# A mixture-of-experts block: the second expert product turned feature-major, with the last 32 tokens gathered by index

## The chip, the cores and the metric

One core of a Trainium2 chip runs the whole program. The metric is device time in microseconds (us) of one execution; the median of three runs of the kernel before is 1306.14 us (1303.92 to 1308.4).

## The reference, cut to what matters

Two transformer blocks of 256 tokens and 1024 features, all in float32. The first ends in a product-key expert layer: each token picks, in each of 8 heads, 16 of 16384 experts. An expert is a row of `u` and a row of `v`; the token's own features are `xb`.

```python
expert = take_along_axis(cand_i, best_pos)            # t, h, k
gate = softmax(best_s)                                # t, h, k
act = gelu(einsum('thkd,td->thk', u[expert], xb))
return einsum('thk,thkd->td', gate * act, v[expert])
```

The second block reads the sum x + peer_ffn(h): a projection `w_in_2` into five parts, attention, a gated unit, `w_out_2`, two layer norms and a SwiGLU.

## The kernel before

The expert layer is computed densely. An expert is numbered by i (128 values) and j (128 values). The U loop goes over 64 pairs of j. For each j it loads a 512 KB slice of `u`, multiplies it with the 256 normed tokens held feature-major in `h2h`/`h2l` (`fm`, 24 matmuls of 256 columns), applies Gelu and keeps the result in `store0`/`store1` with i on the partitions and the tokens on the free axis. Beside that loop, bit by bit, a list `bg` of steps finds the top 16 of each head (`scores` to `slots`), and from pair 22 on `one_hots` and `g_chunk` build, 8 tokens at a time, the dense gate matrix of those tokens: 16 matmuls in f16, multiplied into the store. There are 32 such chunks.

The V loop then goes over the same 64 pairs of j. For each j it loads a 512 KB slice of `v` (128 experts on the partitions, 1024 features) and adds store-times-v to two PSUM accumulators `acc`, one for each block of 128 tokens. The stored values are the stationary operand and the rows of `v` the moving one: the sum stands token-major, tokens on the partitions.

Every float32 product is made of three matmuls in `mm3` (L101 to L103). A value is split into a high part in float32r and the rest: high by high, high by low, low by high. For a streamed slice the split is done in `load` (L84 to L96): SP starts the DMA into one of four `raw` buffers, ScalarE copies it to `wh` (L94), VectorE subtracts to get `wl` (L95). There are six buffers for `wh` and `wl`, so three slices can be ready. The split of the stored values is in `split` (L127 on ScalarE, L128 on VectorE).

The last four slices of `v` (VLAST) and three slices of `w2` are kept in `held`. After the loop, block 0 is finished first (4 slices, 24 matmuls), added to `x1` on VectorE (L806), transposed on TensorE and split into `xh`/`xl`, while block 1's last 24 matmuls run; then the first quarter of the projection (`tm`, 48 matmuls into `qp`) follows.

Instructions are laid out by a tile framework. Each engine has one queue in order; the framework orders it by program order, with the two conversions in `load` moved ahead by 20 places (`ahead`), and sets all semaphores. GpSimd (POOL) starts no DMA in this kernel and has no work between 196 and 1020 us.

Of the kernel before, what the change touches and what calls it, by code (L numbers as in the profile page):

```python
# [18 lines left out]
P = 128  # L19
# [21 lines left out]
AHEAD = 20  # L41
VLAST = 4
FFIRST = 4
WLAST = 4
# [3 lines left out]
def block_kernel(ctx, tc, a, out):  # L48
# [30 lines left out]

    ahead = [AHEAD_MIX]  # L80


    def load(src, dst=None, parts=1):
# [6 lines left out]
        for i in range(parts):  # L90
            c = slice(i * 1024 // parts, (i + 1) * 1024 // parts)
            nc.sync.dma_start(raw[:, c], src[:, c])
            with tc.high_priority(offset=ahead[0]):
                act.activation(wh[:, c], raw[:, c], AF.Copy)  # L94
                dve.tensor_sub(wl[:, c], raw[:, c], wh[:, c].bitcast(F32))  # L95
        return wh, wl  # L96
# [421 lines left out]
    pp = peer_cm.__enter__()  # L518
    store0 = pp.tile([P, 64, S], F32, tag="store", bufs=2, name="store0")
    work = pp.tile([P, 64, S], F32, tag="store", bufs=2, name="work")  # L520
    wf = work.rearrange("p a b -> p (a b)")
# [23 lines left out]
    eq = wf[:, 0:2048].bitcast(F16).rearrange("p (g a s) -> p g a s", g=16, a=16)  # L545
    fi = carve(256)
    fj = carve(256)
    iota16 = carve(128, F16).rearrange("p (a s) -> p a s", s=TOPK)

    iT = pp.tile([P, S], F16, name="iT")  # L550
    jT = pp.tile([P, S], F16, name="jT")
# [90 lines left out]
    def select(q, half):  # L642
# [8 lines left out]
        for w in (8, 4, 2):  # L651
            dve.tensor_tensor(e[:, :, 0:w], e[:, :, 0:w], e[:, :, w:2 * w], op=ALU.add)
        dve.tensor_tensor(dst.rearrange("p (g s) -> p g s", s=TOPK)[:, g], e[:, :, 0, :],
                          e[:, :, 1, :], op=ALU.add)

    def slots(b):
        pt = bank("ms").rearrange("p (k n) -> p k n", n=P)
# [10 lines left out]
    state = {"pairs": 0, "chunks": 0, "hots": 0}  # L668
    hots = []
    stores = [store0, None]  # L670

    def store_view(j0, n, t):
        s = stores[j0 // 64]
        return s[:, j0 % 64:j0 % 64 + n, t]

    def u_pair():
        jp = state["pairs"]
        if jp == 32 and stores[1] is None:
            stores[1] = pp.tile([P, 64, S], F32, tag="store", bufs=2, name="store1")
        pq = bank_s("mm")  # L680
# [8 lines left out]
        if done < S:  # L689
            act.activation(store_view(2 * jp, 2, slice(done, S)), pq[:, :, done:S], AF.Gelu)  # L690
        state["pairs"] += 1
# [20 lines left out]
    def g_chunk():  # L712
        c = state["chunks"]
        if stores[1] is None:
            stores[1] = pp.tile([P, 64, S], F32, tag="store", bufs=2, name="store1")
        ea, el, eb = hots.pop(0)
# [30 lines left out]
    bg += [(4, lambda q=q, h=h: select(q, h)) for h in range(2) for q in range(2)]  # L747
    bg += [(0, lambda: slots(0)), (2, lambda: slots(1))]
    total = sum(w for w, _ in bg)
# [15 lines left out]

    acc = [pair() for _ in range(NB)]
    held = pp.tile([P, 16, 1024], F32R, tag="store", bufs=2, name="held2")

    def v_mm(j, unit, sp, jj, b):
# [7 lines left out]
    xh, xl = across()  # L777
    late = []
    for jp in range(npairs):
        sv = store_view(2 * jp, 2, slice(0, S))  # L780
        if 2 * (npairs - jp) <= VLAST:
            o = 2 * VLAST + npairs - jp - 1
            sp = held[:, o, :].rearrange("p (q j t) -> p q j t", q=2, t=S)
        else:
            sp = pp.tile([P, 2, 2, S], F32R, tag="e", bufs=2, name="sp")
        ph, pl = sp[:, 0], sp[:, 1]
        split(ph, pl, sv)
        for jj in range(2):
            j = 2 * jp + jj
            n = 128 - j - 1  # L790
            if n >= VLAST:
                unit = load(a["v"][j])
                for b in range(NB):
                    v_mm(j, unit, (ph, pl), jj, b)
            else:
                late.append((j, load(a["v"][j], (held[:, 2 * n], held[:, 2 * n + 1])), (ph, pl), jj))
    w2 = a["w2"]
    n = 2 * VLAST + VLAST // 2
    first_q = [load(w2[i], (held[:, n + 2 * i], held[:, n + 2 * i + 1]) if i < 3 else None)
               for i in range(4)]  # L800
    for b in range(NB):
        for item in late:
            v_mm(*item, b)
        for half in range(2):
            c = slice(512 * half, 512 * half + 512)
            dve.scalar_tensor_tensor(x1[:, b, c], acc[b][:, half, :], 1.0 / GSCALE, x1[:, b, c],  # L806
                                     op0=ALU.mult, op1=ALU.add)
        transposed_split(x1[:, b], xh, xl, b, KD)
    qp = pair()
    for b in range(NB):  # L810
        for i in range(4):
            tm(first_q[i], 2 * i, [qp[:, 0, :], qp[:, 1, :]], xh, xl, blocks=[b])
    peer_cm.__exit__(None, None, None)
# [438 lines left out]
```

## Time and profile before

| what | value |
|---|---|
| median of 3 runs | 1306.14 us (1303.92 to 1308.4) |
| the profiled execution, its own time | 1306.18 us |
| its span, from the first to the last instruction | 1304.3 us |
| TensorE busy | 1279.4 us, 98% of the span |
| VectorE busy / ScalarE busy | 853.0 us, 65% / 708.9 us, 54% |
| GpSimd busy | 29.7 us, 2% |
| moved by DMA | 229.12 MB, mean 176 GB/s |
| granted TensorE clock, mean | 0.996 of 2.4 GHz |

A busy TensorE is not yet one at its peak, since matmuls overlap and the ends of their records are modelled. What a matmul costs is read from the distance between the starts of neighbours in the timeline. A group's mean duration (389 ns for a matmul of 512 columns) is longer than that distance and must not be added up.

### The profile page before, as it was taken

How to read it: one execution, taken by the hardware profiler on the slowest of the kernel's cores; microseconds unless marked ns; L12 is line 12 of the kernel's file. 1: busy time of each engine (PE TensorE's matmuls, PEld its weight loads, DVE VectorE, ACT ScalarE, POOL GpSimd, SP SyncE). 2: the span in 40 equal slices, each digit the busy share in tenths (PEclk: the TensorE clock that was granted, in tenths of full speed). 3: DMA queues.
4: the chain of work that ended last, by engine and by line, in shares of the span. 5: the costliest groups of instructions: out<-in, count | busy, mean ns of one | idle time of the engine just before them, and what ended most of it. 6: DMA issues, size and time to landing. Idle time of an engine off the chain costs nothing. (4 is left out here: it accounts for less than half of the span.)

```text
span 1304.3 us, 21924 instructions
## 1 busy us (share of the span) xinstructions
PE 1279.4 (98%) x8644; PEld 1164.7 (89%) x8644; DVE 853.0 (65%) x1454; ACT 708.9 (54%) x1167; POOL 29.7 (2%) x40
## 2 busy tenths in 40 slices
PE   8999999999999999999999999999999999999997
PEld 7998989999999999999988888888887887899996
DVE  5656685499987777777655555555556687554556
ACT  6555454444568777777544444544444475344443
POOL 2200000000000000000000000000000110000000
PEclk9989999999999999999999999999999999999999
DMA  8523555555555444454555565555556564355552
GB/s 301 193 67 99 177 193 182 178 162 162 167 162 190 152 162 158 162 162 162 179 193 194 194 194 193 194 193 194 193 194 216 194 219 137 114 192 180 193 182 94
DMA packets 65479, 229.12 MB, mean 176 GB/s; under 512 B 8288, under 2 KB 9056, under 8 KB 65248
## 3 DMA queue, kind: packets, MB, share of 16 engines
q1 hardware_dynamic: 64800, 226.54, 52.5%
q8 instruction: 68, 1.11, 0.3%
q10 hardware_dynamic: 576, 1.18, 0.3%
q14 instruction: 35, 0.29, 0.1%
HBM read 226.64 MB, written 1.05 MB: 175 GB/s over the span
## 5 line engine op out<-in xcount | busy, mean ns | idle before, releaser
L95 DVE TENSOR_TENSOR wl<-raw,wh 128x1024 fp32r<-128x1024 f32 (+1 forms) x385 | 469.2, 1221 | 322.8 <-ACT wh L94 321.5
L94 ACT ACTIVATE wh<-raw 128x1024 fp32r<-128x1024 f32 (+1 forms) x385 | 405.1, 1054 | 434.3 <-PE ps_lg L102 211.8
L101 PE MATMUL ps_mm<-xh,wh 128*128 128x256 f32 x1408 | 401.8, 285 | 0.0
L103 PE MATMUL ps_mm<-xh,wl 128*128 128x256 f32 x1408 | 398.6, 283 | 2.1 <-DVE wl L95 2.1
L102 PE MATMUL ps_mm<-xl,wh 128*128 128x256 f32 x1408 | 398.3, 283 | 0.0
L103 PEld LDWEIGHTS ps_mm<-xh,wl 128*128 128x128 f32 x1408 | 269.9, 192 | 2.7 <-DVE wl L95 2.7
L102 PEld LDWEIGHTS ps_mm<-xl,wh 128*128 128x128 f32 x1408 | 270.1, 192 | 0.7
L101 PEld LDWEIGHTS ps_mm<-xh,wh 128*128 128x128 f32 x1408 | 269.8, 192 | 0.7
L101 PE MATMUL ps_lg<-wh,sp 128*128 128x512 f32 x496 | 193.0, 389 | 0.0
L102 PE MATMUL ps_lg<-wl,sp 128*128 128x512 f32 x496 | 193.0, 389 | 0.0
L103 PE MATMUL ps_lg<-wh,sp 128*128 128x512 f32 x496 | 192.9, 389 | 0.0
L103 PEld LDWEIGHTS ps_lg<-wh,sp 128*128 128x128 f32 x496 | 93.1, 188 | 19.5
L101 PEld LDWEIGHTS ps_lg<-wh,sp 128*128 128x128 f32 x496 | 93.1, 188 | 19.3
L102 PEld LDWEIGHTS ps_lg<-wl,sp 128*128 128x128 f32 x496 | 93.1, 188 | 19.2
L705 ACT ACTIVATE oh<-oh,gL 128x128 f16<-128x128 f16 x256 | 83.6, 429 | 2.2 <-DVE oh L703 1.9
L101 PE MATMUL ps_mm<-hh,wh 128*128 128x256 f32 x192 | 56.5, 294 | 0.0
L103 PE MATMUL ps_mm<-hh,wl 128*128 128x256 f32 x192 | 55.7, 290 | 0.3 <-DVE wl L95 0.3
L102 PE MATMUL ps_mm<-hl,wh 128*128 128x256 f32 x192 | 55.1, 287 | 0.0
L128 DVE TENSOR_TENSOR sp<-store,sp 128x512 fp32r<-128x512 f32 x62 | 42.4, 683 | 0.2 <-ACT sp L127 0.2
L127 ACT ACTIVATE sp<-store 128x512 fp32r<-128x512 f32 x62 | 38.0, 613 | 0.4 <-DVE store L732 0.4
L101 PEld LDWEIGHTS ps_mm<-hh,wh 128*128 128x128 f32 x192 | 37.4, 195 | 1.0 <-DVE gates L402 0.4
L103 PEld LDWEIGHTS ps_mm<-hh,wl 128*128 128x128 f32 x192 | 37.3, 195 | 0.8 <-DVE wl L95 0.7
(387 smaller groups left out, 1679.0 us busy)
## 6 DMA issues: line engine op xcount, KB each, us to landing
raw<-in_u_dram SPq DMA_DIRECT2D x128, 512.0 KB, 3.3
raw<-in_v_dram SPq DMA_DIRECT2D x128, 512.0 KB, 3.3
raw<-in_wgu_dram SPq DMA_DIRECT2D x44, 512.0 KB, 3.3
raw<-in_wa_dram SPq DMA_DIRECT2D x32, 512.0 KB, 4.2
raw<-in_wd_dram SPq DMA_DIRECT2D x22, 512.0 KB, 3.3
raw<-in_w_dram SPq DMA_DIRECT2D x20, 512.0 KB, 4.4
raw<-in_wo_dram SPq DMA_DIRECT2D x16, 512.0 KB, 3.8
raw<-in_wq_dram SPq DMA_DIRECT2D x16, 512.0 KB, 4.3
```

What stands on the lines that cost most here:

```text
L94: act.activation(wh[:, c], raw[:, c], AF.Copy)
L95: dve.tensor_sub(wl[:, c], raw[:, c], wh[:, c].bitcast(F32))
L101: pe.matmul(dst, lh, rh, start=start, stop=False)
L102: pe.matmul(dst, lh, rl, start=False, stop=False)
L103: last_mm[0] = pe.matmul(dst, ll, rh, start=False, stop=stop)
L127: act.activation(dh, src, AF.Copy)
L128: dve.tensor_sub(dl, src, dh.bitcast(F32))
L705: act.activation(el[:, t // 2, :, t % 2], ea[:, t // 2, :, t % 2], AF.Copy, scale=gL[:, GT * c + t:GT * c + t + 1])
```

## The change

The dense path now covers tokens 0 to 223 (NT = 224). The last 32 (NR) go another way from the Gelu on; the U product is still made for all 256.

- **V loop, turned round.** For each j and each of 8 blocks of 128 features (d) there are two matmuls in place of twelve over two token blocks: `wh` of that block is the stationary operand and the moving one is high and low part of the 224 tokens side by side (448 columns); then `wl` is stationary and the high part alone moves (224 columns). The sums stand feature-major in eight PSUM banks, columns 0 to 223 and 224 to 447, and use all of PSUM.
- **U loop.** 28 chunks in place of 32. One more Gelu for each pair, of the last 32 tokens, into `last_u`; every fourth pair ScalarE starts a DMA of it to a buffer in HBM, `kept_u` (16 DMAs).
- **New steps in the list.** `row_numbers` (VectorE) computes the 4096 expert numbers of the 32 tokens, GpSimd moves them with 4 DMAs into an order in which each partition holds one token's 32 slots, VectorE reads them back. `across_x1` transposes `x1` into `x1T` (16 transposes, 4 ScalarE copies).
- **Gather.** During the V loop GpSimd issues 32 indexed DMAs of 128 x 32 values from `kept_u` and 32 indexed DMAs of 128 rows of `v` (512 KB each). VectorE picks the values and weighs them (`weigh`, 4 times 3 instructions), then multiplies and adds each row into `rows_sum` (`add_row`, 32 instructions of 128x1024). All of these VectorE instructions are queued behind the last `wl` of their pair (`issue_after`).
- **End.** For each d: one float32 matmul of 32 columns brings `rows_sum` into columns 448 to 479 of the bank, eight matmuls of the four kept slices follow, then two ScalarE copies, two VectorE instructions and a split. No transposes are needed before the projection; after its first quarter 16 transposes bring `x1` back token-major. The `w2` slices are no longer kept in `held`.

```diff
+NT = 224
+NR = S - NT
+ROWS = 4
+U_FIRST = 5
+V_FIRST = 18
+V_LAST = 60
...
+    def row_numbers():
+        t = slice(P, 2 * P)
...
+        dve.scalar_tensor_tensor(pack[:, 0, :], fj[:, t], float(NKEYS), fi[:, t], op0=ALU.mult,
+                                 op1=ALU.add)
...
+            pool.dma_start(prep[r], pack[P - NR:P, :, r])
+        dve.tensor_copy(index, prep[:, 0:2, :])
...
     def u_pair():
...
+        act.activation(last_u[0][:, 2 * k:2 * k + 2, :], pq[:, :, NT:S], AF.Gelu)
+        if k == 3:
+            act.dma_start(kept_u[:, 2 * jp - 6:2 * jp + 2, :], last_u[0])
...
-        nch = S // GT
+        nch = NT // GT
...
-    acc = [pair() for _ in range(NB)]
...
+    def fetch_u(c):
+        at_u = pp.tile([P, 8, NR], F32, tag="last_u", bufs=2, name="at_u")
+        for i in range(8):
+            r = 8 * c + i
+            pool.indirect_dma_start(at_u[:, i, :], None, table,
+                                    bass.IndirectOffsetOnAxis(ap=index[:, 1, r:r + 1], axis=0))
...
+    def fetch_row(r):
+        pool.indirect_dma_start(place(r), None, vrows,
+                                bass.IndirectOffsetOnAxis(ap=index[:, 0, r:r + 1], axis=0))
+
+    def add_row(r):
...
+            dve.scalar_tensor_tensor(rows_sum, place(r), share[:, r:r + 1], rows_sum,
+                                     op0=ALU.mult, op1=ALU.add)
+
+    def steps(jp):
+        if jp == 0:
+            fetch_u(0)
+            fetch_u(1)
+        for c in range(4):
+            if jp == U_FIRST + 3 * c:
+                weigh(c)
+                if c < 2:
+                    fetch_u(c + 2)
...
+        for r in range(NR):
+            if jp == V_FIRST + r * (V_LAST - V_FIRST) // NR:
+                add_row(r)
+                if r + ROWS < NR:
+                    fetch_row(r + ROWS)
...
+    acc = [bank("ms"), bank("ms"), lgs[0][:, 0, :], lgs[0][:, 1, :], lgs[1][:, 0, :],
+           lgs[1][:, 1, :], bank("mm"), bank("mm")]
...
+    def v_mm(j, unit, sp, d):
         wh, wl = unit
-        t = slice(b * P, b * P + P)
-        for half in range(2):
-            c = slice(512 * half, 512 * half + 512)
-            mm3(acc[b][:, half, :], sp[0][:, jj, t], sp[1][:, jj, t], wh[:, c], wl[:, c],
-                j == 0, j == 127)
+        c = slice(P * d, P * d + P)
+        pe.matmul(acc[d][:, 0:2 * NT], wh[:, c], sp.rearrange("p q t -> p (q t)"), start=j == 0,
+                  stop=False, skip_group_check=True)
+        pe.matmul(acc[d][:, 0:NT], wl[:, c], sp[:, 0], start=False, stop=j == 127,
+                  skip_group_check=True)
...
+        with tc.issue_after(last_wl[0]):
+            steps(jp)
...
+    for d in range(KD):
+        c = slice(P * d, P * d + P)
+        pe.matmul(acc[d][:, 2 * NT:2 * NT + NR], rows_sum[:, c], mine, start=False, stop=True,
+                  skip_group_check=True)
+        for item in late:
+            v_mm(*item, d)
...
+        dve.tensor_tensor(both[:, 0:NT], both[:, 0:NT], acc[d][:, 0:NT], op=ALU.add)
+        dve.scalar_tensor_tensor(y, both, 1.0 / GSCALE, y, op0=ALU.mult, op1=ALU.add)
+        split(xh[:, d, :], xl[:, d, :], y)
```

## Rows read from the trace of the kernel before

**Rows 1.** The page: the span, the busy time of each engine, and the granted TensorE clock in 40 equal slices.

```profile
span 1304.3 us, 21924 instructions
PE 1279.4 (98%) x8644; PEld 1164.7 (89%) x8644; DVE 853.0 (65%) x1454; ACT 708.9 (54%) x1167; POOL 29.7 (2%) x40
PEclk9989999999999999999999999999999999999999
```

**Rows 2.** The table by stretch. Columns: the stretch and its length, busy us of each engine with its instructions, granted clock, DMA share, GB/s. In order: the top-k part of the U loop, the end of the U loop, the V loop, the end of the expert layer, the start of the program.

```profile
300.00:400.00 100.00, 97.87 (x835) 97.01 (x834) 88.96 (x285) 56.67 (x97) 0.00 (x0) 1.00 0.53 171
...
600.00:640.00 40.00, 40.00 (x367) 39.83 (x366) 29.70 (x38) 25.61 (x54) 0.00 (x0) 1.00 0.53 171
...
652.30:989.60 337.30, 337.30 (x1490) 279.28 (x1489) 191.96 (x189) 166.88 (x190) 0.00 (x0) 1.00 0.59 196
984.00:1000.00 16.00, 14.31 (x68) 11.73 (x67) 11.56 (x11) 9.08 (x9) 0.00 (x0) 1.00 0.87 310
0.00:33.00 33.00, 27.73 (x173) 24.93 (x174) 19.70 (x38) 22.88 (x40) 7.67 (x12) 1.00 0.84 297
```

**Rows 3.** TensorE's timeline (start us, us of one, operation): the last slice of the U loop (21 matmuls from the first of these rows to the second), the first matmul of the V loop, the first after it.

```profile
649.78 0.28 PE L101 MATMUL ps_mm<-xh,wh 128*128 128x256 f32 x1
...
652.18 0.28 PE L103 MATMUL ps_mm<-xh,wl 128*128 128x256 f32 x1
652.30 0.40 PE L101 MATMUL ps_lg<-wh,sp 128*128 128x512 f32 x1
...
989.60 0.39 PE L101 MATMUL ps_lg<-held 128*128 128x512 f32 x1
```

**Rows 4.** TensorE's timeline where the moving operand is short: 64 columns in float32 (24 in a row), 128 columns in float32 (6 in a row), and 128 columns in float32r (the attention logits, two matmuls at a time on 64 partitions each; nine steps from the first of these two rows to the last).

```profile
1067.62 2.79 PE L999 MATMUL ps_lg<-v,ptt 128*128 128x64 f32 x24
...
212.95 0.83 PE L573 MATMUL ps_ms<-work 128*128 128x128 f32 x6
...
1034.12 0.27 PE L152 MATMUL ps_lg<-qkL,qkH 64*128 64x128 f32 x2
...
1035.12 0.27 PE L152 MATMUL ps_lg<-qkL,qkH 64*128 64x128 f32 x2
```

**Rows 5.** TensorE's timeline across one chunk of the gate matrix in the U loop, 16 matmuls in f16, with its neighbours.

```profile
542.58 0.28 PE L103 MATMUL ps_mm<-xh,wl 128*128 128x256 f32 x1
542.70 0.23 PE L719 MATMUL ps_lg<-oh 128*128 128x128 f16 x1
...
543.57 0.22 PE L721 MATMUL ps_lg<-oh 128*128 128x128 f16 x1
...
543.80 0.28 PE L102 MATMUL ps_mm<-xl,wh 128*128 128x256 f32 x1
```

**Rows 6.** TensorE's timeline across four transposes and the second matmul after them.

```profile
206.33 0.60 PE L562 MATMUL ps_ms<-ident,qtok 128*128 128x128 f32 x4
...
206.89 0.28 PE L102 MATMUL ps_mm<-xl,wh 128*128 128x256 f32 x1
```

**Rows 7.** Groups by line in the V loop, 652.3 to 989.6 us: count, busy us, mean ns of one, and the idle time of the engine before them with what ended it.

```profile
L95 DVE TENSOR_TENSOR wl<-raw,wh 128x1024 fp32r<-128x1024 f32 x122 | 149.5, 1226 | 143.7 <-ACT wh L94 143.7
L94 ACT ACTIVATE wh<-raw 128x1024 fp32r<-128x1024 f32 x122 | 129.5, 1061 | 168.8 <-PE ps_lg L102 167.0 <-PE ps_mm L102 1.8
...
L128 DVE TENSOR_TENSOR sp<-store,sp 128x512 fp32r<-128x512 f32 x60 | 41.0, 683 | 0.0
```

**Rows 8.** Single lines elsewhere (ns of one: least, median, most): a VectorE multiply-add with both operands in SBUF, and the two halves of a split of 256 columns.

```profile
L1038 DVE SCALAR_TENSOR_TENSOR xc<-x,lst,l1g x4: 736/742/746, 1100.1 to 1113.3; 128x512 f32<-128x512 f32 x4
...
L127 ACT ACTIVATE f<-sg x18: 398/398/420, 1141.4 to 1286.0; 128x256 fp32r<-128x256 f32 x18
...
L128 DVE TENSOR_TENSOR f<-sg,f x18: 417/421/426, 1142.7 to 1286.5; 128x256 fp32r<-128x256 f32 x18
```

**Rows 9.** TensorE's timeline at the end of the expert layer: the last matmul before the wait, the transposes of block 0 with the wait before them, the first matmul of `qp`, the first after `qp`.

```profile
996.63 0.39 PE L102 MATMUL ps_lg<-held 128*128 128x512 f32 x1
998.70 0.65 PE L135 MATMUL ps_ms<-ident,x 128*128 128x128 f32 x4 [1.69 <-DVE x L806]
...
1003.30 0.39 PE L101 MATMUL ps_lg<-held,xh 128*128 128x512 f32 x1
...
1015.21 0.39 PE L101 MATMUL ps_lg<-wh,xh 128*128 128x512 f32 x1
```

**Rows 10.** ScalarE's and VectorE's timelines just after the U loop: the last pair leaves its PSUM bank.

```profile
653.34 0.58 ACT L686 ACTIVATE ps_mm<-ps_mm 128x512 f32<-128x512 f32 x1
...
654.61 0.68 DVE L688 TENSOR_TENSOR store<-store,ps_mm 128x512 f32<-128x512 f32 x1
```

**Rows 11.** DMAs: a slice of `v` and a piece of the output (size, median us from issue to landing), and the time that SP takes to issue one slice (ns, least, median, most).

```profile
raw<-in_v_dram SPq DMA_DIRECT2D x128, 512.0 KB, 3.3
...
out_dram<-ot SPq DMA_DIRECT2D x4, 256.0 KB, 2.1
...
L92 SPq DMA_DIRECT2D raw<-in_v_dram x128: 327/328/328, 637.5 to 982.8; - x128
```

**Rows 12.** GpSimd's timeline: two of its instructions on tiny operands.

```profile
28.07 2.10 POOL L264 TENSOR_TENSOR hst<-hst,neghalf 128x5 f32<-128x5 f32 x1
...
188.72 0.56 POOL L142 TENSOR_TENSOR st<-st,neghalf 128x1 f32<-128x1 f32 x1 [110.64 <-DVE st L141]
```

More of the change, by code (lines that the diff above doesn't have):

```diff
@@ L747, in block_kernel @@
     bg += [(4, lambda q=q, h=h: select(q, h)) for h in range(2) for q in range(2)]
-    bg += [(0, lambda: slots(0)), (2, lambda: slots(1))]
+    bg += [(1, row_numbers), (0, lambda: slots(0)), (2, lambda: slots(1))]
+    bg += [(0, lambda b=b: across_x1(b)) for b in range(NB)]
     total = sum(w for w, _ in bg)
@@ L764, in block_kernel @@
             g_chunk()
[L766 to L777 removed]
+    table = kept_u.rearrange("p j t -> (p j) t")
@@ new lines, in block_kernel @@
+    vrows = a["v"].rearrange("j i d -> (j i) d")
+    places = [h2pool.tile([P, 2, 1024], F32, tag=t, name="rows") for t in ("xh", "xl")]
+    fetched = []
+    def fetch_u(c):
[4 more added lines that the diff above has]
+                                    bass.IndirectOffsetOnAxis(ap=index[:, 1, r:r + 1], axis=0))
+        fetched.append(at_u)
@@ new lines, in weigh, with place @@
+    def weigh(c):
+        at_u = fetched[c]
+        r = slice(8 * c, 8 * c + 8)
+        dve.tensor_tensor(at_u, at_u, mine[:, None, :].to_broadcast([P, 8, NR]), op=ALU.mult)
+        dve.tensor_reduce(share[:, r], at_u, axis=AX.X, op=ALU.add)
+        dve.tensor_tensor(share[:, r], share[:, r], prep[:, 2, r], op=ALU.mult)
+    def place(r):
+        return places[r % ROWS // 2][:, r % 2, :]
+    def fetch_row(r):
+        pool.indirect_dma_start(place(r), None, vrows,
+                                bass.IndirectOffsetOnAxis(ap=index[:, 0, r:r + 1], axis=0))
@@ new lines, in block_kernel @@
+    lgs = [pair() for _ in range(2)]
+    acc = [bank("ms"), bank("ms"), lgs[0][:, 0, :], lgs[0][:, 1, :], lgs[1][:, 0, :],
+           lgs[1][:, 1, :], bank("mm"), bank("mm")]
+    held = pp.tile([P, 14, 1024], F32R, tag="store", bufs=2, name="held2")
+    def v_mm(j, unit, sp, d):
+        wh, wl = unit
+        c = slice(P * d, P * d + P)
[3 more added lines that the diff above has]
+                  skip_group_check=True)
@@ L792, in block_kernel @@
                 unit = load(a["v"][j])
-                for b in range(NB):
-                    v_mm(j, unit, (ph, pl), jj, b)
-            else:
-                late.append((j, load(a["v"][j], (held[:, 2 * n], held[:, 2 * n + 1])), (ph, pl), jj))
+                for d in range(KD):
+                    v_mm(j, unit, sp[:, jj], d)
+            else:
+                late.append((j, load(a["v"][j], (held[:, 2 * n], held[:, 2 * n + 1])), sp[:, jj]))
+        with tc.issue_after(last_wl[0]):
+            steps(jp)
@@ L797, in block_kernel @@
+    xh, xl = across()
     w2 = a["w2"]
-    n = 2 * VLAST + VLAST // 2
-    first_q = [load(w2[i], (held[:, n + 2 * i], held[:, n + 2 * i + 1]) if i < 3 else None)
-               for i in range(4)]
-    for b in range(NB):
[L802 to L812, printed above, removed]
+    for d in range(KD):
+        c = slice(P * d, P * d + P)
[3 more added lines that the diff above has]
+            v_mm(*item, d)
+        y = x1T[:, d, :]
+        both = pp.tile([P, S], F32, tag="last_u", bufs=2, name="both")
+        act.activation(both[:, 0:NT], acc[d][:, NT:2 * NT], AF.Copy)
+        act.activation(both[:, NT:S], acc[d][:, 2 * NT:2 * NT + NR], AF.Copy)
+        dve.tensor_tensor(both[:, 0:NT], both[:, 0:NT], acc[d][:, 0:NT], op=ALU.add)
+        dve.scalar_tensor_tensor(y, both, 1.0 / GSCALE, y, op0=ALU.mult, op1=ALU.add)
+        split(xh[:, d, :], xl[:, d, :], y)
@@ L813, in block_kernel @@
+    qp = pair()
+    for i in range(4):
+        tm(load(w2[i]), 2 * i, [qp[:, 0, :], qp[:, 1, :]], xh, xl)
+    for b in range(NB):
+        for g in range(2):
+            pt = bank_t("ms")
+            for i in range(4):
+                pe.transpose(pt[:, i, :], x1T[:, 4 * g + i, b * P:b * P + P], ident)
+            act.activation(x1[:, b, 512 * g:512 * g + 512].rearrange("p (k n) -> p k n", n=P), pt,
+                           AF.Copy)
     peer_cm.__exit__(None, None, None)
```

63 lines of the change are left out of this document (49 added, 14 removed).

## Prediction

> **What bounds the kernel now.** I read the page first: TensorE is busy 98% of the span, VectorE 65%, ScalarE 54%, GpSimd 2%, and the granted clock is 9 or more tenths of full speed in all slices but one [rows 1]. So time is gained only where TensorE has fewer or shorter matmuls, and lost where it begins to wait. The table by stretch says the same of each stage: in the V loop TensorE is busy for all of 337.3 us, VectorE for 57% of it, ScalarE for 49%, and the DMA engines for 0.59 [rows 2]. What TensorE pays for a matmul is read from the starts in its timeline. The V loop runs 124 slices of 12 matmuls between 652.30 and 989.60 us [rows 3]: 2.720 us a slice, 226.7 ns for 512 columns. The U loop runs 20 steps between 649.78 and 652.18 us [rows 3]: 120.0 ns for 256 columns. A line through both has 0.4167 ns a column (which is 2.4 GHz, the clock granted there) and 13.3 ns for each matmul. In the groups by line VectorE and ScalarE sit idle for 144 and 169 us in the V loop, and what ends this idleness is TensorE giving a `wh`/`wl` buffer back [rows 7]. Nothing there is late for TensorE.
>
> **Part 1, the V loop.** Per slice 12 matmuls of 512 columns go; 8 of 448 and 8 of 224 columns come: 5376 streamed columns in place of 6144, but 16 weight loads in place of 12. The 448-column matmul lies between the two measured sizes: 448 x 0.4167 + 13.3 = 200.0 ns. The 224-column one lies below both, and the next weights must be in by then. The line alone gives 106.7 ns. 64 columns in float32 take (2.79 - 0.27)/23 = 109 ns, 128 take (0.83 - 0.27)/5 = 112 ns (0.27 us is the length of one record), and the float32r logits of 128 columns 1.00/9 = 111 ns a step [rows 4]. Half the columns are not cheaper, while f16 with 128 columns takes 0.87/15 = 58 ns [rows 5]. So there is a floor near 110 ns under 32-bit matmuls that is not their columns; I read it as the weight load. From above the 256-column matmul bounds it, 120.0 ns. I take 112, the row nearest in size that shows the floor. A slice is then 8 x (200.0 + 112) = 2.496 us, 0.224 us less; over 124 slices **-27.8 us**, with ends of -33.1 (106.7 ns) and -19.9 (120.0 ns).
>
> A page of the Trainium skill, "TensorE: Matmul & The Clock Gate", section "LDWEIGHTS (loading the stationary operand)", gives a load as columns over 1.2 GHz, 106.7 ns for 128; the rows' floor is 2 to 5 ns above that. By the page the loop would gain 33.1 us, and the forecast would be 5 us lower.
>
> **Part 2, what must stay under the loop.** A pair of slices then lasts 4.99 us. VectorE has two `wl` (2 x 1.226 us) and one split (0.68 x 448/512 = 0.60) [rows 7], and in 32 of the 42 pairs from 18 to 59 one `add_row`. A multiply-add of 512 columns takes 742 ns [rows 8]; doubled, less one fixed part of about 0.2 us, 1.3 us. Together 4.35 of 4.99 us: it fits. ScalarE has 2 x 1.061 + 0.55 = 2.7 us. A `wl` that comes behind a split and an `add_row` is ready about 1.06 + 0.60 + 1.30 + 1.23 = 4.2 us after its buffer is freed, and TensorE has two more slices ready, 4.99 us. I cost VectorE's 32 adds at nothing; cover gone, each would cost up to its 1.3 us. DMA: 512 KB per 2.496 us is 210 GB/s, and one gathered row of 512 KB each 42 x 4.99/32 = 6.55 us is 80 more. 290 GB/s is wanted; 310 and 297 flowed where the loads were pressed [rows 2]. It fits by 7%; a load has some 8 us to land and needs 3.3 now [rows 11]. The short matmuls of `rows_sum` cost 8 x 0.11 = 0.9 us (in part 4). GpSimd's queue is empty until 1020 us, so the gathers pass nobody there; behind a late gather, though, `weigh` or `add_row` holds VectorE, the next `wl` waits, then TensorE. That is rival C.
>
> **Part 3, the U loop.** Four of 32 chunks go. A chunk shifts the stream by 543.80 - 0.12 - 542.70 = 0.98 us [rows 5]: -3.9 us. Four groups of transposes come, each 206.89 - 0.12 - 206.33 = 0.44 us [rows 6]: +1.8. `row_numbers` makes VectorE wait for GpSimd's four small DMAs, behind which the `wl` of the stream are queued, in the stretch where VectorE is already busy 89% and TensorE loses 2.1 us [rows 2]. A DMA takes 2.1 to 3.3 us to land [rows 11], four issues on GpSimd lie between 0.3 [rows 11] and 2.1 us each [rows 12], so the wait is some 3 to 10 us, of which the two ready slices (5.8 us here, less 2.3 of conversion) hide 3.5. I take 1 us, ends 0 and 4. The 64 extra Gelus and 16 DMA issues on ScalarE, at most 0.3 us each, stand against 32 fewer chunk copies; ScalarE is 64% busy at the end of the loop [rows 2], and no one waits. At the seam the eighth accumulator is the bank of the last pair. VectorE leaves it at 654.61 + 0.68 = 655.3 us now [rows 10]; the first matmul on it would come at 652.30 + 7 x 0.312 = 654.5: +0.8 us, ends 0 and 1.5. Sum of part 3: **-0.3 us**, ends -2.1 and +3.4.
>
> **Part 4, the end of the layer.** Now it lasts from 989.60 to 1015.21, 25.6 us, with 1.8 us of waiting for the add to `x1` before 998.70 [rows 3, 9]. After: eight times four slices and one short matmul, 8 x (4 x 0.312 + 0.11) = 10.9; the projection as now without its transposes, 1015.21 - 1003.30 - 2 x 0.44 = 11.0 [rows 6, 9]; 16 transposes back, 1.8. For each d VectorE has three instructions of some 0.42 us, ScalarE a split, a copy of 224 and a copy of 32 columns, about 1.0 [rows 8]: less than the 1.36 us of TensorE, but the conversions of `w2` (1.23 us each) come between. The last block needs some 2.5 us after its matmul; the projection reaches its slice of x only after 7/8 of 11 us, so that hides it. For what remains I take 1 us, ends 0 and 3. 24.7 in place of 25.6: **-0.9 us**, ends -1.9 and +1.1.
>
> **The sum.** -27.8 - 0.3 - 0.9 = -29.0 us. The profiled execution took 1306.18 us, 1.9 more than its span and within 0.1 of the median of 1306.14, so no correction is due: **1277 us**. All ends together give 1269 and 1291.
>
> **The rivals.**
> (B) The gathered rows make DMA the bound. For: 290 GB/s is near what the loads reached, and nothing in this trace gathers by index. Against: the rows are 4 KB like those of a slice. At 270 GB/s the 210 us with gathers stretch by 7%: +16, 1293 us. If a gathered row takes twice a plain row's engine time, 370 GB/s are wanted of 310: +41, 1318 us.
> (C) Issuing on GpSimd is slow: the side of slower. The first 32 gathers are due in steps of 8 per three pairs, 14.97 us, so one may take 1.87 us. An issue costs 0.33 us on SP [rows 11], and GpSimd spends 0.56 to 2.1 us on tiny operands [rows 12]. Every microsecond above 1.87 stops VectorE, then TensorE, 32 times: at 2.5 us +20, 1297 us; above 1.87 + 29.0/32 = 2.8 us the kernel is slower than before; at 4 us 1345 us. I expect 1 to 1.5 us, between the two engines' rows.
> The Trainium skill, "SBUF — State Buffer", section "Who interferes with whom", says that a VectorE instruction with two SBUF inputs holds the port that a GpSimd instruction reading SBUF needs. In the V loop VectorE would work some 80% of the time on such instructions, each 0.6 to 1.3 us. If an indexed DMA reads its indices that way, an issue gets up to 1.3 us longer and lands between the two prices of C. The page infers that building descriptors needs the write side alone; no run here shows either.
> (D) The short pass does not get cheaper: 224 columns in float32r run at half rate. Four times slower is excluded, since 128 columns at a step of 111 ns leave no room for 213 [rows 4], but half rate is not, as it gives 107. Then 224 columns take 200 ns, a slice 3.20 us, +60 in the loop: 1361 us. Against: 64 columns need the same 109 ns [rows 4], so half rate is not needed to explain the floor.
> (E) The change does what it says, but the new steps in the U loop stall more often than once, a wait of 10 us and one of 5: 1290 us.
>
> **How the numbers follow.** Forecast 0.64; B 0.09 (mild) and 0.04 (hard); C 0.07 (1297, of which 0.02 within the bound of no change) and 0.07 (slower); D 0.05; E 0.04. A measurement of this kernel can tell 0.3%, some 4 us, from no change. Faster: 0.64 + 0.09 + 0.05 + 0.04 = 0.82. Same 0.02. Slower: 0.04 + 0.07 + 0.05 = 0.16. The forecast's own range is 1269 to 1291. Reaching up to the mild B and C (1293, 1297) leaves out B hard, C slow and D; below, 2 us more for a floor that is a little lower: 1267 to 1299.
>
> **What would show it.** After: matmuls of 448 columns start 200 ns and those of 224 columns 107 to 120 ns before the next; the V loop takes 124 x 2.50 = 309 us, not 337; VectorE's wait before `wl` is still ended by ScalarE, and ScalarE's by TensorE, not by a DMA. GpSimd's issues stand closer than 1.87 us. It is wrong if 224 columns take 200 ns (D), if `weigh` waits for `at_u` (C), if `wh` waits for `raw` in pairs 18 to 59 (B), or if TensorE idles in the U loop near 360 to 400 us (E).

## The result, and the profile after

The changed kernel takes 1292.45 us, median of 4 (1289.65 to 1293.69), beside 1306.43 for the kernel before on the same chip: ratio 0.9891, 95% interval 0.9867 to 0.9915. That is 14.0 us faster where I forecast 29: the direction was right and the time lies inside the range, but the gain is less than half of the forecast. The page of the profiled execution (1293.11 us), against [rows 1]:

```profile
span 1291.4 us, 23149 instructions
...
PE 1258.8 (97%) x9124; PEld 1184.4 (92%) x9124; DVE 884.0 (68%) x1502; ACT 706.7 (55%) x1222; POOL 119.8 (9%) x108
...
PEclk9989999999999999999999999999999999999999
```

TensorE works 20.6 us less, but the span is only 12.9 us shorter: part of what was saved came back as waiting. The windows tell where (columns as in [rows 2]): the first us of the V loop, its undisturbed part, its last 10 us, and the beginning of the late phase, as I call the stretch from the loop's end to the projection.

```profile
650.00:660.00 10.00, 9.08 (x63) 8.46 (x62) 4.66 (x5) 4.85 (x8) 4.52 (x4) 1.00 0.75 255
660.00:700.00 40.00, 40.00 (x254) 37.80 (x254) 25.36 (x30) 20.18 (x24) 27.70 (x28) 1.00 0.76 253
700.00:950.00 250.00, 250.00 (x1581) 236.23 (x1580) 188.41 (x189) 128.48 (x152) 56.08 (x33) 1.00 0.77 267
...
962.00:968.00 6.00, 3.77 (x21) 2.82 (x19) 4.54 (x6) 3.78 (x4) 0.00 (x0) 1.00 0.77 259
968.00:972.00 4.00, 3.95 (x15) 3.67 (x16) 2.40 (x2) 1.64 (x2) 0.00 (x0) 0.57 0.81 259
972.00:976.00 4.00, 4.00 (x29) 3.86 (x28) 2.72 (x3) 1.87 (x4) 0.00 (x0) 1.00 0.97 320
```

For 300 us TensorE never waits, though VectorE adds rows and GpSimd gathers. At 962 it runs dry, and at 968 the granted clock falls to its lower level (0.57 in that row). TensorE's timeline has the borders and each wait (the number in brackets): the V loop from 652.12 to 972.04 (319.92 us; before 337.30, [rows 3]), the late phase with `rows_sum` and the kept slices to 987.18, `qp` to 998.10. From one pair of matmuls to the next it is 316.65 ns in the mean (124 slices of 2.533 us).

```profile
652.12 0.37 PE L880 MATMUL ps_ms<-sp,wh 128*128 128x448 f32 x1
...
930.05 0.38 PE L880 MATMUL ps_lg<-sp,wh 128*128 128x448 f32 x1
930.27 0.27 PE L882 MATMUL ps_lg<-sp,wl 128*128 128x224 f32 x1
930.37 0.38 PE L880 MATMUL ps_lg<-sp,wh 128*128 128x448 f32 x1
...
963.10 0.48 PE L880 MATMUL ps_ms<-sp,wh 128*128 128x448 f32 x1 [0.58 <-DVE sp L135]
...
966.60 0.47 PE L880 MATMUL ps_ms<-sp,wh 128*128 128x448 f32 x1 [0.72 <-ACT wh L101]
968.05 0.37 PE L882 MATMUL ps_ms<-sp,wl 128*128 128x224 f32 x1 [0.98 <-DVE wl L102]
...
972.04 0.31 PE L909 MATMUL ps_ms<-mine,rows_sum 128*128 128x32 f32 x2
...
979.40 0.41 PE L909 MATMUL ps_lg<-mine,rows_sum 128*128 128x32 f32 x2 [1.93 <-DVE both L917]
...
983.82 0.41 PE L909 MATMUL ps_lg<-mine,rows_sum 128*128 128x32 f32 x2 [0.89 <-DVE both L917]
...
987.18 0.40 PE L108 MATMUL ps_lg<-wh,xh 128*128 128x512 f32 x1
...
998.10 0.71 PE L927 MATMUL ps_ms<-ident,x1T 128*128 128x128 f32 x5
```

The groups by line between 656 and 962 us answer to [rows 7]: what ends ScalarE's idle time is still TensorE, and VectorE's is ScalarE, with 39.7 us of row adds fitted in. The issue of a row gather takes GpSimd 1.78 us in the mean, but GpSimd idles three times as long.

```profile
L102 DVE TENSOR_TENSOR wl<-raw,wh 128x1024 fp32r<-128x1024 f32 x120 | 147.1, 1225 | 81.4 <-ACT wh L101 78.1
...
L101 ACT ACTIVATE wh<-raw 128x1024 fp32r<-128x1024 f32 x120 | 127.3, 1061 | 144.5 <-PE ps_mm L880 143.3 <-DMA raw<-in_v_dram 1.2
...
L841 POOL DMA_INDIRECT rows<-in_v_dram,index x30 | 53.3, 1776 | 168.4 <-DVE rows_sum L848 128.4 <-DVE rows_sum L846 39.4 <-issue 0.6
...
L848 DVE SCALAR_TENSOR_TENSOR rows_sum<-rows,share,rows_sum 128x1024 f32<-128x1024 f32 x31 | 39.7, 1279 | 0.0
```

And ScalarE's timeline has what goes wrong before 962 us: the conversion of a kept slice (`held`) stands 3.14 us waiting for its own DMA, and the next `wh` of the stream is behind it in ScalarE's queue.

```profile
954.85 1.06 ACT L101 ACTIVATE wh<-raw 128x1024 fp32r<-128x1024 f32 x1 [1.00 <-PE ps_mm L880]
959.05 1.06 ACT L101 ACTIVATE held<-raw 128x1024 fp32r<-128x1024 f32 x1 [3.14 <-DMA raw<-in_v_dram]
960.02 1.05 ACT L101 ACTIVATE wh<-raw 128x1024 fp32r<-128x1024 f32 x1
```

The way from the forecast of -29.0 to the span's -12.9, in us: the V loop starts 0.2 earlier (forecast 1.1): +0.9. The loop is 17.4 shorter, forecast 27.0 with its seam (the change from the U to the V loop): +9.6. The end of the layer grew by 2.3 (15.14 + 10.92 + 1.8 against 25.6), forecast -0.9: +3.2. What remains, 0.4, was lost in the next layer. And from VectorE's last instruction (ended at 1286.40) to the end of the span 5.0 us pass, where before it was 3.0 (1301.28 to 1304.3): +2.0.

### The profile page after: what moved, and what is told of

Its sections match the earlier page's. It is cut to its first block, busy times and chain, and to the rows that moved or that the text cites. A ratio compares the mean times of both kernels' runs of the same rounds, so it can differ in the third digit from the quotient of the medians.

```text
span 1291.4 us, 23149 instructions
## 1 busy us (share of the span) xinstructions
PE 1258.8 (97%) x9124; PEld 1184.4 (92%) x9124; DVE 884.0 (68%) x1502; ACT 706.7 (55%) x1222; POOL 119.8 (9%) x108
## 5 line engine op out<-in xcount | busy, mean ns | idle before, releaser
L880 PE MATMUL ps_lg<-sp,wh 128*128 128x448 f32 x496 | 165.5, 377 | 0.0
L882 PE MATMUL ps_lg<-sp,wl 128*128 128x224 f32 x496 | 132.2, 267 | 0.0
L880 PEld LDWEIGHTS ps_lg<-sp,wh 128*128 128x128 f32 x496 | 93.5, 189 | 8.7
L841 POOL DMA_INDIRECT rows<-in_v_dram,index x32 | 55.9, 1747 | 445.7 <-PE ps_mm L110 277.1
L882 PEld LDWEIGHTS ps_lg<-sp,wl 128*128 128x128 f32 x496 | 95.3, 192 | 0.0
L880 PE MATMUL ps_mm<-sp,wh 128*128 128x448 f32 x248 | 86.5, 378 | 0.9 <-ACT last_u L738 0.9
L880 PE MATMUL ps_ms<-sp,wh 128*128 128x448 f32 x248 | 86.1, 376 | 1.3 <-ACT wh L101 0.7
L882 PE MATMUL ps_ms<-sp,wl 128*128 128x224 f32 x248 | 66.0, 266 | 1.0 <-DVE wl L102 1.0
L882 PE MATMUL ps_mm<-sp,wl 128*128 128x224 f32 x248 | 66.0, 266 | 0.0
L880 PEld LDWEIGHTS ps_ms<-sp,wh 128*128 128x128 f32 x248 | 46.5, 188 | 6.1 <-ACT wh L101 1.0
```

What stands on the lines that cost most here:

```text
L841: pool.indirect_dma_start(place(r), None, vrows, bass.IndirectOffsetOnAxis(ap=index[:, 0, r:r + 1], axis=0))
L880: pe.matmul(acc[d][:, 0:2 * NT], wh[:, c], sp.rearrange("p q t -> p (q t)"), start=j == 0, stop=False, skip_group_check=True)
L882: pe.matmul(acc[d][:, 0:NT], wl[:, c], sp[:, 0], start=False, stop=j == 127, skip_group_check=True)
```

## The experiments

Times are medians with the ratio to the kernel before on the same chip. On which chip a run was made a difference, so it is named: e1 to e4 ran on chip 5, e5 to e8 on chip 0, e9 to e16 on chip 8; for the first run of the changed kernel the chip is not known.

**e1, e2, e4: accumulator halves, early loads, no gathers.** e1 maps the blocks of 128 features to other halves:

```
acc = [lgs[0][:, 0, :], lgs[1][:, 0, :], bank("ms"), bank("ms"), lgs[0][:, 1, :],
       lgs[1][:, 1, :], bank("mm"), bank("mm")]
```

> The accumulators of two consecutive blocks of 128 features no longer share one two-bank tile (blocks 0 and 4, and 1 and 5, share one; nothing else changes). Theory: in the changed kernel the short matmul of block 3 waits 1.93 us and that of block 5 0.89 us for VectorE to read the other half of their tile, 2.8 us in all, out of 15.14 us between the last matmul of the V loop and the first of the projection. With other halves these waits go: some 12.3 us there, the kernel 2.8 us faster than the changed one, near 1289.6 us. Rival: VectorE and ScalarE are too slow in this stretch with the conversions of w2 between the blocks; then the wait only moves to a later block or to the start of the projection, and less than 1 us is won.

The late phase took 12.36 us, as expected, and TensorE has no wait left in it:

```profile
986.92:999.28 12.36, 12.36 (x83) 11.89 (x81) 8.71 (x19) 5.35 (x19) 0.00 (x0) 0.95 0.48 174
```

But the run took 1299.1 us (median of six executions; for a seventh see the last section; 0.9939, 0.9923 to 0.9956), 9.5 us more than expected: between 677 and 699 us, which the edit doesn't touch, TensorE idled 12 us ("the stop", see e13).

e2 loads the late slices at `jp in LATE_AT = (36, 41, 46, 51)`, before that pair's own slices.

> The four slices that are kept for the late phase are loaded at pairs 36, 41, 46 and 51 instead of at pairs 62 and 63; the rest stays. Theory: at the end of the V loop eight slices must come in the time of four, the raw buffers can't turn over so fast, ScalarE stands at a kept slice's conversion for a DMA (3.14 us) with the next wh behind it, TensorE runs dry three times (2.3 us) and its granted clock then falls to 0.50 for 3.5 us. With the loads spread out no gap over 0.3 us and no granted clock below 0.95 between 955 us and the end of the loop: 4 to 5 us faster than the changed kernel, near 1288 us, with nothing lost at pairs 36 to 51. Rival: the gathered rows hold the DMA engines, so extra loads in the middle of the loop stall TensorE there by as much; then below 1 us is won.

1309.59 us (1.0017, 0.9998 to 1.0036). Beside the stop, TensorE has three new waits of 2.9, 0.9 and 2.9 us at 847, 902 and 929 us. ScalarE's timeline gives the cause of the first:

```profile
839.21 1.06 ACT L102 ACTIVATE wh<-raw 128x1024 fp32r<-128x1024 f32 x1 [1.00 <-PE ps_mm L881]
845.75 1.06 ACT L102 ACTIVATE held<-raw 128x1024 fp32r<-128x1024 f32 x1 [5.48 <-DMA raw<-in_v_dram]
846.71 1.04 ACT L102 ACTIVATE wh<-raw 128x1024 fp32r<-128x1024 f32 x1
```

A kept slice needs no `w` buffer, so its conversion is queued as soon as its load is issued, ahead of slices that have landed: the `wh` behind it follows without a wait. Moving the load moves the blockade with it. The rival has a part in its length: from 836 to 842 us the DMA engines were at 0.92. e3, e1 and e2 together (expected 1285), had 11.80 us in the late phase, waits of the same kind in the loop, the stop, and 1308.46 us (1.0027, 1.0008 to 1.0045).

e4 drops `steps(jp)`, and with it all gathers and row adds, and sets `rows_sum` to zero.

> Leaves out all indexed DMAs, their weighing and the 32 row adds: the second product of the last 32 tokens is zero. Everything else, the steps in the U loop among it, is as in the changed kernel. Theory: the gathers lie wholly under TensorE, so the pace of the loop stays 316.65 ns a pair of matmuls and the V loop as long as it is, within 1 us, and the late phase too: 1292 us, within 1.5. Rival: the gathers and adds take the missing gain (DMA engines at 0.8, VectorE at 0.78): then the loop gets shorter by 4 us or more, above all its starved end, 1288 us or less.

1289.29 us (0.9881, 0.9862 to 0.99). The loop took 318.51 us, starved at its end as before: the gathers neither set its pace nor starve its end. The late phase took 16.73 us, 1.6 more than in the first run (e5 has 17.03 with the gathers). On this chip e1 to e3 had the stop; e4, without gathers, has none. The time is below the expected band by 1.2 us: from VectorE's last instruction to the end of the span it has 3.06 us, as the kernel before, in place of 5.0.

**e5 to e8: the order of the conversions.** e5 is the changed kernel again, to see whether the stop comes in it too.

> The changed kernel itself once more, beside the next three on their chip. In the three runs before this that gather, the plain loads stopped for 5 to 16 us between 676 and 698 us, while 24 to 28 small gathers of at_u were issued one every 1.25 us; in the first run of the changed kernel the same burst stopped nothing. Theory (the stop belongs to the burst and comes in some executions): this run has it too, in its trace or in its times, and the median is 1296 to 1300 us. Rival (the stop comes from the other edits): 1292 us as before, and no load over 6 us in the trace.

1290.22 us (0.9883, 0.9863 to 0.9904), no stop. The rival, that the other edits make the stop, is refuted by e13. e5's V loop took 317.36, its late phase 17.03: the starvation is smaller than in the first run and the late wait larger, 7.3 us together in place of 8.0 (over 315.2, which is 124 slices of 2.533 and the seam, and 11.9).

e6 queues a kept slice's conversions behind the last `wh` and `wl` of the stream (shortened):

```
+ with tc.issue_after(behind[0]), tc.issue_after(behind[1]):
      last_wh[0] = act.activation(wh[:, c], raw[:, c], AF.Copy).ins
      last_wl[0] = dve.tensor_sub(wl[:, c], raw[:, c], wh[:, c].bitcast(F32)).ins
```

> The conversions of the four kept slices are queued on ScalarE and VectorE behind that of the last slice of the stream; their loads stay where they are. Theory: the end of the V loop starves because the conversion of a kept slice, which needs no wh buffer, is queued ahead of the conversions of two earlier slices and waits there for its own DMA (3.14 us). With the order of the slices kept, no gap over 0.4 us and no granted clock of 0.50 between 955 us and the last slice of the stream: 4 us less than the run of the changed kernel beside it. Rival: the loads themselves come too late, in whatever order they are converted; then the gap only moves to the first matmul on a kept slice, and less than 1.5 us is won.

The loop ended without a gap, 315.30 us; the 0.92 us without work are the seam's:

```profile
649.28:964.58 315.30, 314.38 (x1986) 296.91 (x1985) 228.68 (x233) 163.02 (x190) 87.32 (x64) 1.00 0.77 263
```

So the cause of the starved end is shown. But the late phase took 18.88 (a wait of 3.96 us for `both`, granted clock 0.82), and the run 1289.64 us (0.9884, 0.9863 to 0.9906). Against e5 nothing was won where 4 us were expected; the wait had only changed its place, though not to the one that the rival named.

e7 gathers `at_u` in fours, eight at the start and four at each weighing.

> The 32 small gathers of at_u come in groups of four, two groups at the start and one more at each weighing, every second pair (10.1 us), instead of groups of eight back to back. The same is computed. Theory of the burst: a stop of the plain loads needs many gathers on end; with at most eight on end there is none, no load takes over 6 us, and the run is as long as the changed kernel in an execution without a stop, 1290 to 1292 us, whatever the run of the changed kernel beside it gives. Rival: what stops the loads is not the density of the gathers; then the loads still stop, in a longer stretch, and the time is that of the unchanged kernel beside it or more.

1292.73 us (0.9902, 0.9881 to 0.9924) on a chip where e5 had no stop either: it tells nothing of the stop. It has one wait of its own: the first weighing, now at pair 3, holds VectorE 3.92 us for a gather, and TensorE waits 1.14 us for the split behind it. That is rival C, in small.

> The edits of e1, e6 and e7 together: accumulator halves of consecutive blocks apart, kept slices converted in their order, small gathers in fours. Theory: each removes its own stall (2.8, 4 and whatever the burst costs): 1284 to 1286 us. If the late phase has another limit behind the wait that e1 removes, 1287 to 1289 us.

1287.8 us (0.9859, 0.9839 to 0.9878), loop 316.58, late phase 13.68: the second case of the expectation. TensorE, which needs 1.47 us a block, still waits 0.45 us for `both` before block 4 and 0.32 us before the projection. VectorE comes to block 0 late, at 972.86 us, behind a kept slice's conversion and three of `w2`, and then is slower than TensorE. VectorE's timeline, blocks 1 to 3:

```profile
974.52 0.38 DVE L922 TENSOR_TENSOR both<-both,ps_lg 128x224 f32<-128x224 f32 x1
974.94 0.42 DVE L923 SCALAR_TENSOR_TENSOR x1T<-both,x1T 128x256 f32<-128x256 f32 x1
...
976.19 0.38 DVE L922 TENSOR_TENSOR both<-both,ps_ms 128x224 f32<-128x224 f32 x1
...
977.86 0.38 DVE L922 TENSOR_TENSOR both<-both,ps_ms 128x224 f32<-128x224 f32 x1
```

ScalarE's timeline beside it:

```profile
975.39 0.42 ACT L138 ACTIVATE xh<-x1T 128x256 fp32r<-128x256 f32 x1 [0.92 <-DVE x1T L923]
975.72 0.34 ACT L920 ACTIVATE both<-ps_ms 128x224 f32<-128x224 f32 x1
975.96 0.19 ACT L921 ACTIVATE both<-ps_ms 128x32 f32<-128x32 f32 x1
977.06 0.42 ACT L138 ACTIVATE xh<-x1T 128x256 fp32r<-128x256 f32 x1 [0.92 <-DVE x1T L923]
```

1.67 us a block: the split waits 0.92 us for VectorE's add, the copies of the next block stand behind the split, and VectorE's next add waits for those copies. Neither engine is full; they take turns. Alone this costs TensorE nothing: in e1 and e3 VectorE's blocks come every 1.67 us too, and TensorE does not wait.

**e9, e10: the pace.** In e9 the short matmul has half of its columns: `acc[d][:, 0:112]` and `sp[:, 0, 0:112]` stand in L882. e10 makes two passes over d, first all long matmuls of a slice, then all short ones.

> The short matmul of the V loop takes 112 columns in place of 224 (the low part of the second product is left out for half of the tokens); the kept slices keep 224. In the changed kernel a long and a short matmul take 316.65 ns together, where I forecast 312. Theory (weight load: the short step sits on a floor under 32-bit matmuls and its columns cost nothing): the pair stays at 316 to 317 ns, the loop as long as it was. Rival (columns: 224 columns cost more than the floor and the rest is a fixed part of each matmul): the pair falls by up to 112 x 0.4167 = 46.7 ns, to 270 ns; between the two, what is left of the fall measures how far above the floor 224 columns lie.

TensorE's timeline, five pairs:

```profile
929.76 0.42 PE L880 MATMUL ps_ms<-sp,wh 128*128 128x448 f32 x1
930.03 0.21 PE L883 MATMUL ps_ms<-sp,wl 128*128 128x112 f32 x1
...
931.33 0.42 PE L880 MATMUL ps_mm<-sp,wh 128*128 128x448 f32 x1
```

Over 160 pairs a pair takes 313.4 ns. Half of the short one's columns, 46.7 ns by the 0.4167 ns a column, save 3.3: a pair stands on a floor that is not the short one's columns, as I read from [rows 4]. Which of the two steps is dearer than forecast, e9 doesn't tell: here a long one starts 262 ns before the next and a short one 52, in the changed kernel 214 and 102. (A single execution, 1301.82 us, with a stop in it.)

> In each slice the eight long matmuls come first and then the eight short ones, in place of long and short by turns. Theory (each matmul has its own price, whatever stands beside it): a slice stays at 2.533 us and the time within 1 us of the changed kernel's 1290.2. Rival (a short matmul hides only 93 ns of the next weight load, so the long one behind it starts late, and by turns each pair pays for that once): with a load behind each long matmul wholly hidden and 105 to 110 ns for a short one, a slice takes 8 x 200 + 8 x 108 = 2.46 us, 8 us less over the loop; if a short one behind a short one is dearer than 117 ns, it is slower.

A slice took 2.52 us, 315 ns a pair: 1.6 us less in the whole loop, so the neighbour hardly matters. Here the two prices stand apart. TensorE's timeline, the first of eight short ones, the first of eight long ones, and the next short one:

```profile
902.27 0.38 PE L884 MATMUL ps_ms<-sp,wl 128*128 128x224 f32 x2
...
903.16 0.58 PE L881 MATMUL ps_ms<-sp,wh 128*128 128x448 f32 x2
...
904.79 0.38 PE L884 MATMUL ps_ms<-sp,wl 128*128 128x224 f32 x2
```

A short one takes 0.89/8 = 111 ns, a long one 1.63/8 = 204. The run took 1302.87 us (0.9965, 0.9944 to 0.9986), with a stop.

**e11, e15, e16: the late order.** On top of e1 and e6, for each block d (shortened):

```
+ if d:  late_split(d - 1, copied.ins, added.ins)   # behind this block's copies and add
+ load(w2[i], behind=w2_behind if i == 2 else None)  # behind block 0
```

> The edits of e1 and e6, and a new order behind them in the late phase: on ScalarE and VectorE the split of a block is queued behind the copies and the adds of the next block, and the third conversion of w2 behind the first block. Theory: in the late phase of e8 a block takes 1.66 us, not TensorE's 1.36, since ScalarE's split waits for VectorE's add, and the copies of the next block stand behind it; out of that order VectorE has 1.26 us a block and TensorE decides. The late phase then takes 11.5 to 12.5 us (13.68 in e8, 17.03 in the changed kernel), the loop 315.3, and the run 1285 to 1286 us. Rival: the conversions of the kept slices and of w2, 2.3 us each, are what VectorE and ScalarE are late with; then the phase stays at 13.5 us or more.

The late phase took 11.95 us: no wait for VectorE is left in it. Whether the new order or the moved conversion of `w2` freed it is not separated. The run took 1297.78 us (0.9938, 0.992 to 0.9955), its loop 322.47 with a stop. e16 repeated it: 11.91, a loop of 329.88 with a stop, 1296.55 us (0.991, 0.9879 to 0.9941), 6.0 less than the unedited kernel beside it (e13), where 4 or more were expected.

> e11 with the small gathers in groups of four, one group for each second pair, weighed from pair 5 on and the row adds from pair 20 on. On a chip that stops the loads: if the density of the gathers decides, no load over 6 us and 1284 to 1286 us; if any small gather can stop them, they stop as in the runs beside it, 1290 us or more. On a chip that doesn't: as e11 within 1.5 us.

1285.58 us (0.9834, 0.9812 to 0.9855), beside e16 on the same chip 11 us less: the shortest of all the runs. Windows of e15, the loop and the late phase: TensorE has no idle time in the second.

```profile
652.25:968.40 316.15, 314.64 (x1986) 297.03 (x1985) 229.79 (x245) 162.74 (x190) 89.57 (x64) 1.00 0.78 262
968.40:980.19 11.79, 11.79 (x82) 11.36 (x81) 10.59 (x22) 7.99 (x23) 0.00 (x0) 1.00 0.74 258
```

**e13: the stop.** The unedited changed kernel on chip 8.

> The changed kernel a third time, to see it beside the next three on their chip. On two chips every run with the small gathers (e1 to e3, e9 to e12) had plain loads that took 5 to 16 us between 676 and 698 us; on two others none had (the first run of the changed kernel, e5 to e8). Theory: this is the chip, not the edits: where the three runs beside it stop, this one stops too (1296 to 1300 us), and where they don't, it takes 1290 to 1292 us. Rival: the changed kernel itself never stops.

1302.58 us (0.9981, 0.996 to 1.0003; 1296 to 1300 expected): on this chip the change as it is gains nothing that is clear of noise. Its windows, where the first run had TensorE at 100% and clock 1.00:

```profile
660.00:670.00 10.00, 10.00 (x65) 9.47 (x64) 5.84 (x7) 5.17 (x6) 7.68 (x7) 1.00 0.88 306
670.00:680.00 10.00, 7.95 (x49) 7.34 (x48) 2.17 (x3) 1.53 (x2) 7.62 (x8) 0.97 0.47 142
680.00:690.00 10.00, 8.29 (x30) 7.41 (x29) 5.91 (x8) 5.17 (x6) 6.58 (x6) 0.52 0.43 119
```

ScalarE's timeline in that stretch; "remote" is a releaser that the profile doesn't show, and what it waits for is a `raw` whose load SP issued long before (that of the first row at 665.37):

```profile
680.29 1.06 ACT L101 ACTIVATE wh<-raw 128x1024 fp32r<-128x1024 f32 x1 [6.29 <-remote]
683.96 1.06 ACT L101 ACTIVATE wh<-raw 128x1024 fp32r<-128x1024 f32 x1 [2.61 <-remote]
```

The DMA engines are at 0.43, so it isn't their bandwidth. Late loads are not the whole of it either: in e1 10.8 of the 12.0 us for which TensorE idles in the stop are put down to "issue", a wait for nothing that the profile shows, and 8.9 of them (682.1 to 696.9 us) lie within one slice, whose `wh` and `wl` TensorE was already using. Whether the engines' own instructions come late was not tested. And part of the loss is the granted clock, 0.52 in the third row. The same stretch of e16, with the gathers back to back, and of e15, in fours:

```profile
680.00:690.00 10.00, 5.48 (x17) 4.01 (x17) 1.76 (x2) 1.64 (x2) 7.87 (x8) 0.65 0.28 79
```

```profile
680.00:690.00 10.00, 10.00 (x65) 9.44 (x65) 6.91 (x11) 5.04 (x7) 4.98 (x4) 1.00 0.82 268
```

e15 and e16 differ in the grouping of the small gathers and in the pairs of the weighings and row adds that follow from it. So on this chip a burst of 24 or so small gathers, one every 1.25 us, comes with the stop, and groups of four, at most eight on end, do not (one wait of 0.59 us is left).

**e12, e14: the end of the program.** One half of the gathers each.

> Keeps the 32 small gathers of at_u and their weighing, leaves out the 32 gathers of rows and the row adds (the second product of the last 32 tokens is zero). In the runs with all gathers 5.0 us pass between VectorE's last instruction and the end of the span, in the kernel before and in e4, without any, 3.0 to 3.1, though the last store lands at the same distance. Theory: 2.0 us are the price at the end of the program for having used indexed DMAs at all: 5.0 here too. Rival: it grows with their number or bytes: 3.1 to 4.1 us. The pace of the loop should be 316.65 ns a pair as in both.

> Leaves out the 32 small gathers of at_u (a zero in their place, so the second product of the last 32 tokens is zero); the 32 gathers of rows and their adds stay. End of the program: with all 64 gathers 5.0 us pass between VectorE's last instruction and the end of the span, with the 32 small ones alone 3.1, with none 3.06. If the 2.0 us belong to the gathers of rows: 5.0 here; if to the number of gathers on the queue: 3.1. Stop of the loads: by the theory that the small gathers make it, none here on any chip, and no granted clock below 0.98 from 655 to 955 us.

VectorE's last instruction in e12 (span 1296.8), and in e14 (span 1296.5):

```profile
1292.28 1.41 DVE L1158 SCALAR_TENSOR_TENSOR ot<-xc,lst,l2b 128x512 f32<-128x512 f32 x2 [0.44 <-POOL lst L1153]
```

```profile
1292.03 1.42 DVE L1162 SCALAR_TENSOR_TENSOR ot<-xc,lst,l2b 128x512 f32<-128x512 f32 x2 [0.44 <-POOL lst L1157]
```

From its end to the end of the span it is 3.1 us in both: neither kind alone costs anything, both together, 64 gathers, cost 2.0. Whether it is the number or the two kinds together was not tried. e12 kept the pace of 316.7 ns and had a stop without any row gather (1298.49 us); e14 had none without the small gathers, but its zeroing of `at_u` made VectorE wait 7.8 us for `kept_u`, which cost TensorE a wait of 3.07 us and a lower clock after it, so its 1298.25 us tell nothing. Both are single executions.

## Why the prediction was right in sign and half in size

Three terms of the sum failed: the price of a pair in part 1 (4.6 us), the ends of the loop in part 2, which I put at nothing without a reason (4.7 us), and the late phase in part 4 (3.2 us). 2.0 us at the end of the program were in no term.

**Part 1, the pace** (right mechanism, wrong size): a pair takes 316.65 ns, not 200 + 112 = 312: 124 x 8 x 4.65 ns = 4.6 us of the missing gain. In e10, where equal ones stand together, the short one costs 111 ns, close to the forecast, and the long one 204, not the 200 of my line; that is 3.0 of the 4.65, and taking them by turns costs the other 1.65. The starts that I named as a sign, 200 and 107 to 120 ns, did not come (214 and 102): only their sum can be read there. The price by the Trainium skill ("TensorE: Matmul & The Clock Gate", section "LDWEIGHTS (loading the stationary operand)"), 106.7 ns, is further off: 23.2 us came where it gives 33.1. Rival D is out with the pair at 316.65 ns; its time adds up to 1364 us, not 1361.

**Part 2, what hides under the loop:** right for the 300 us in the middle: no wait, so B and C are out (gathers issued in 0.94 to 1.99 us, VectorE busy for 188 of 250 us). It failed at the end of the loop, which I had not costed. At the last pairs four kept slices come besides the stream, their conversions are let in early, and in-order queues stand at them: 4.7 us, of which 2.3 are waits, with the granted clock at its lower level behind them. e6 shows the cause: with the conversions in order the loop takes 315.3. In the kernel before ScalarE waited for kept slices too, but at most 1.46 us and behind the last `wh` of the stream (981.42 us):

```profile
986.75 1.06 ACT L94 ACTIVATE held<-raw 128x1024 fp32r<-128x1024 f32 x1 [1.46 <-DMA raw<-in_v_dram]
```

**Part 2, the small gathers:** I priced GpSimd's issuing and the bytes, but not what a burst does to other queues. In the measured run it did nothing; on chips 5 and 8 it lengthened the profiled loops by some 7 to 20 us, and the median by 12.4 (e13 against e5). None of the rivals was this. What does it is open: these runs show that it comes with the small gathers alone (e12) and not without them (e14, e4), that in groups of four they don't bring it (e15 against e16), and that it did not come on chip 0 (the chip and the time at which it was used are not apart). The Trainium skill ("DMA: Bandwidth & Descriptors", section "Queues, rings and completion order") has each DMA engine take turns among queues, a packet at a time. By that, as an estimate, the gathers, 0.31 MB from 670 to 700 us in e13 beside 4.46 MB of loads, could not hold a load for 6 us on engines at 0.43.

**Part 3, U loop and seam:** 1.1 forecast, 0.2 in the first run; but the V loop of the unedited changed kernel started at 652.1, 650.0 and 649.1 in three runs, so 0.9 is within what one profile can tell. The seam cost 1.07 where I said 0.8.

**Part 4, the late phase** (the step that failed worst for its size): I took 1 us for the waits, ends 0 and 3, on the ground that a block costs VectorE 1.26 us of TensorE's 1.36. The matmuls alone take 11.8, not 10.9 (e15): the float32 matmul of 32 columns costs 0.21 us, not 0.11 (11.8 less 32 pairs, by eight). And the waits were 2.8 to 4.0 (first run, e5, e6, e13). Their cause is shown: two neighbouring blocks share one accumulator tile, so TensorE's next write waits for VectorE's read of the other half, and with other halves the wait is gone (e1, e3). It is as long as it is because VectorE comes late and takes 1.67 us a block, by turns with ScalarE; with e1's halves that limits TensorE only where the conversions come late as well (e8; e11 frees it). Busy sums can't see either.

**The end of the program:** 2.0 us not foreseen (e12, e14, e4: they come only with all the gathers; why stays open).

4.6 + 4.7 + 0.3 (the seam) in the loop, 3.2 in the late phase, 2.0 at the end, 0.9 before the loop and 0.4 in the next layer make the 16.1 us. Rival E gave 1290 us, nearest to the measured time, but by stalls in the U loop that did not come.

## What to carry to other kernels

Cost the first and last few us of a sped-up loop apart: work let in early (kept buffers, next weights) stands in the same in-order queues, and one early conversion that waits for its load holds back all behind it. Give neighbouring accumulators tiles of their own, so that the next write doesn't wait for a read of the last. For a chain over two engines add up one turn of the cycle, not each engine's busy time, and put a step that waits for the other engine behind the next block's independent steps. Spread small indexed DMAs out (groups of four here), and time a kernel that uses them on more than one chip.

## What was not expected of the hardware

Beside a burst of indexed DMAs of 128 B rows ScalarE waited up to 15.8 us for plain loads of another queue (e1), with the DMA engines at 0.22 to 0.43 from 680 to 690 us and TensorE's matmuls up to 2.1 us apart, on chips 5 and 8 in every kernel with the burst (e1 to e3, e9 to e13, e16) and not on chip 0 (e5, e6). One of seven executions of e1 took 4183.56 us; no trace of it exists, and whether it is the same thing is open. With 64 indexed DMAs the end of the program is 2.0 us longer, with 32 of either kind not. And the granted clock, at 1.00 before, was 0.50 from 968.6 to 972 us, its lower level (1.2 GHz), after three short waits of TensorE, 2.3 us in all, and was back at 1.00 from 972 on.
